# Layer 0's second adaLN round moved from TensorE to two VectorE accumulators

## The chip, the cores and the metric

The kernel runs as one program on one core of one Trainium2 chip. The metric is the device time of one execution in microseconds (us), as the median of several executions. Of the core's engines four matter here: TensorE (PE, matrix products into PSUM), VectorE (DVE, elementwise), ScalarE (ACT, elementwise and exponentials), and the SyncE queue (SP), which issues the loads from HBM. Each engine works through its own instruction list in a fixed order; instructions on different engines wait for each other through semaphores.

## The reference

A decoder trunk of two layers over 256 tokens of width 1024. What matters here, cut from the reference:

```python
for l in range(DEPTH):                                  # 2 layers
    mod = jax.nn.silu(c) @ ada_w[l] + ada_b[l]          # c (1, 1024), ada_w (1024, 6144)
    sh_a, sc_a, g_a, sh_m, sc_m, g_m = jnp.split(mod, 6, axis=-1)
    h = x * (1 + sc_a) + sh_a
    parts = jnp.split(h @ w_in[l], SPLIT_POINTS, axis=-1)
    oa = dilated_attention(aq, ak, av, bias_a)                      # group A
    ob, _ = banded_attention(rope(bq), rope(bk), bv, 127, sinks)    # group B
    oc = nsa_attention(cq, ckc, cvc, ..., gates, cmp_w1, cmp_w2)    # group C
    mixed = jnp.concatenate([oa, ob, oc], axis=-1)
    x = layer_norm(DN_ALPHA * x + (1 + g_a) * (mixed @ w_out[l]), ln_g[l, 0], ln_b[l, 0])
    h = x * (1 + sc_m) + sh_m
    f = jnp.square(relu(h @ mlp_w1[l])) @ mlp_w2[l]
    x = layer_norm(DN_ALPHA * x + (1 + g_m) * f, ln_g[l, 1], ln_b[l, 1])
```

`mod` is a vector times a 1024 x 6144 matrix. The kernel computes it in rounds. The round at issue is layer 0's round 2: `sc_m` and `sh_m`, 2048 columns, needed only when the MLP's input `h` is made after the attention.

## The kernel before, in words

**Stages of layer 0.** The input projection runs from the start to about 69 us. Then comes the attention: group C in eight units (0 to 7: one for each half n of the tokens and each pair of heads), its compressed branch (`c` and `C`, fed by `compress`, whose steps are the letter `s`), group B (`b`, `B`) and group A (`E`, `e`), with the remaining projections between them (`a` is the chunk t11, `A` the chunk t13). Then the output projection (`wo`, L1044), a transition that makes the MLP's input, and the MLP. Every weight that is multiplied in full precision is first split into a high and a low part: ACT writes `whi` (L179), DVE writes `wlo` (L180), into the ten buffers of the pool `spl` (tag `w`, L127).

**A unit of attention.** PE makes scores `s` (L680 or L744), DVE adds the bias and takes the extreme (L634), ACT makes exponentials (L636), DVE and ACT scale `P` (L642, L640), PE transposes it (`tp`, L648), ACT copies it out (`pT`, L650), PE multiplies by the values (`acc`), and ACT and DVE write the result's two parts (`mx`, L666 and L667).

**Loads.** `rawload` (L136) takes one of four 1 MB buffers (`raw`, L126) and issues its load on SP. SP issues in program order, so a load whose buffer is not yet free holds up all loads behind it.

**The adaLN rounds.** `gemv` (L202) is a generator. Each step loads 1 MB of the round's weights and multiplies it in. With `dve` set, DVE does it into accumulators of 128 x 1024: the first row block by a tensor-scalar multiplication (L229), each later one by a multiply-add (L234); at the end PE sums the accumulator's 128 partitions with a matmul by ones (L242). Without `dve`, PE does it: four matmuls for each block of 128 rows, each into 32 columns of the array and 512 wide (`gemv_mm`, L167 and L168). Before, layer 0's round 3 (a gate, four steps, one accumulator, `GV[0] = 'v'`) goes to DVE and round 2 (eight steps, `GV[1] = None`) to PE. Both are queued in `fill` (L921), round 3 first.

**What sets the order.** The string `ORDER[0]` lists the attention's jobs by letter; each dot runs one step of the first generator in `fill` (`filler`, L276), and `filler(100)` (L1038) runs what is left. So in layer 0 dots 1 to 4 are the steps of round 3; dot 5 is its end and step 0 of round 2; further dots are the next steps. A list scheduler then lays each engine's instructions out in one fixed order from this, by priorities and its own cost estimates; what stands in that order is printed below in the section on the change.

Of the kernel before, what the change touches and what calls it, by code (L numbers as in the profile page):

```python
# [10 lines left out]
F32 = mybir.dt.float32  # L11
# [8 lines left out]
S, D, DEPTH, FF, N_IN = 256, 1024, 2, 4096, 2584  # L20
# [7 lines left out]
SPARES = (('w', 'P', 'qk'), ('w', 'qk', 'P', 'mx'))  # L28
EARLY = 3
FO = (1, 3)  # L30
ORDER = ('kv0..21s4.3sa5.s.Acb.6.B7C..Ee', '.ts..q0412...ss3s.kva5cb.67AB.E..Ce')
GV = ('v', None, 'v', 'v', 'v')
START = ('r', '', '', '', '', '', 'bpbco', 'b', '')
GROUPS = ((0, 4, 0), (4, 8, 32))

# [85 lines left out]
def trunk_kernel(ctx: ExitStack, tc: tile.TileContext, a):  # L121
# [5 lines left out]
    spl = pool("spl", 10)  # L127
    att = pool("att")
# [73 lines left out]
    def gemv(l, r, dve=None, early=0):  # L202

        gate = r in GATE
        w = 256 if gate else 512
        nk = 2 if gate else 1
        if dve:
            acc = [att.tile([128, D], F32, name="qk", tag="qk", bufs=3) for _ in range(1 if gate else 2)]
        else:
            gv = ps.tile([128, 512], F32, name="gv", tag="pt")  # L210
        ahead = []
# [226 lines left out]
    def load_ln(l, s):  # L438
        t = big.tile([128, 2, D], F32, name="lnb", bufs=1)
        for i, k in enumerate(("ln_g", "ln_b")):  # L440
            src = a[k]
            nc.sync.dma_start(t[:, i], bass.AP(tensor=src.tensor, offset=src.offset + (2 * l + s) * D,
                                               ap=[[0, 128], [1, D]]))
        return t
# [474 lines left out]
    for l in range(DEPTH):  # L919
        nc.vector.tensor_scalar(nsink[l], pp("sink", 4 * l, 4), -1.0, None, op0=OP.mult)  # L920
    fill += [gemv(0, 3, GV[0]), gemv(0, 2, GV[1])]  # L921

    for l in range(DEPTH):
# [66 lines left out]
        else:  # L990
# [6 lines left out]
            def rows(w, dst, scale, step=1):  # L997

                def run(b):
                    t = u2("kr")[:, :256]  # L1000
                    nc.scalar.activation(t, v_tile(w, b, 256), AF.Copy, scale=scale)
                    tp = ps.tile([128, 4, 128], F32, name="tp", tag="acc")
                    for i in range(2):
                        nc.tensor.transpose(tp[:, i], t[:, i * 128:(i + 1) * 128], ident)
                    return lambda: nc.scalar.activation(dst[:, :, b * 128:(b + 1) * 128][:, :, ::step], tp[:, :2], AF.Copy)
                return run

            end = finish((l, 1), before, SPARES[1], (lambda b: vc_out(b, v_tile(ws, b, NVC)), rows(wk, KK, 1.0),
                                                     rows(wq, qC[:, 0:2], QS, -1)))
            fill.append(gemv(1, 3, GV[2]))  # L1010
            with tc.issue_after(end[1]):
                for n in end[2]:
# [22 lines left out]
        jobs["+"] = lambda: next(btab)  # L1035
        for j in ORDER[l]:
            jobs[j]()
# [39 lines left out]
        def m1_rows(g, b):  # L1077

            if b == 0:
                FT[g] = new_f()  # L1080
            o = v_tile(W1[g], b, 256)
            t = u2("fr")
            nc.scalar.activation(t[:, :256], o, AF.Relu)
            nc.scalar.activation(t[:, 256:], t[:, :256], AF.Square)
            tp = ps.tile([128, 4, 128], F32, name="tp", tag="acc")
            for i in range(2):
                nc.tensor.transpose(tp[:, i], t[:, 256 + i * 128:384 + i * 128], ident)
            ts = slice(b * 128, (b + 1) * 128)

            def parts_out():  # L1090
                nc.scalar.activation(FT[g][:, 0, :, ts], tp[:, :2], AF.Copy)
                nc.vector.tensor_tensor(FT[g][:, 1, :, ts], tp[:, :2], FT[g][:, 0, :, ts].bitcast(F32), op=OP.subtract)
            return parts_out
# [14 lines left out]
        def m2(g, b, hs):  # L1108
            f = FT[g]
            t = slice(b * 128, (b + 1) * 128)  # L1110
            for i, h in ((i, h) for i in range(2) for h in hs):
# [9 lines left out]
        end = transition(lambda b, h: [wo(b, c2, h) for c2 in (2, 3)], accs, ROUND[l, 3], lnb, (l, 2), before, SPARES[0],  # L1121
                         [lambda b, g=g: m1_rows(g, b) for g in range(EARLY)])
        fill.append(gemv(l, 4, GV[3]))
        if l == 0:
            fill += [gemv(1, 1, GV[4]), gemv(1, 2, GV[4])]
        lnb = load_ln(l, 1)
# [90 lines left out]
```

## Time and profile before

| | |
|---|---|
| median of 3 executions | 706.01 us (705.96 to 706.22) |
| the profiled execution: its time | 706.43 us |
| the profiled execution: its span, first to last instruction | 704.7 us |
| mean granted TensorE clock | 0.991 of 2.4 GHz |
| attention of layer 0, up to the first `wo` matmul | about 69 us to 156.1 us |

The profile comes from one execution. It gives for each engine its busy time, the chain of work that ended last (followed back from the last instruction through what released each step), the instructions in order of time, and the clock that TensorE was granted. The modelled end of a matmul overlaps the next one's start, so the distance between two starts is the better price of a matmul.

### The profile page before, as it was taken

What the parts mean: (1) busy time and instruction counts of PE and PEld (TensorE: products, weight loads), DVE (VectorE), ACT (ScalarE), POOL (GpSimd) and SP (SyncE); (2) the same over time, 40 slices, a digit from 0 to 9 for tenths busy, and PEclk for the clock granted to TensorE, in tenths of its full rate; (3) what the DMA queues carried; (4) which work ended last, traced back from release to release, by engine and by line L of the source; (5) the groups of instructions that cost most, each with busy time, mean ns of one, the idle gap of its engine ahead of it and who ended that gap; (6) DMA issues with size and microseconds to landing.
All of it is one profiled execution on the core that took longest, in us unless ns stands there. A gap on an engine that the chain in (4) does not pass through costs nothing.

```text
span 704.7 us, 11146 instructions
## 1 busy us (share of the span) xinstructions
PE 674.1 (96%) x4284; PEld 550.9 (78%) x4284; DVE 492.3 (70%) x947; ACT 402.6 (57%) x781; POOL 39.1 (6%) x39
## 2 busy tenths in 40 slices
PE   5998899999999999999998999999999999999994
PEld 4898658458788888888878977867788888888883
DVE  3455965657799879798977976657779855555556
ACT  2345473785665546656555447598474655656550
POOL 0000000000400000000013020000220000000003
PEclk9999999999999999999999999999999999999998
DMA  9998686568459989798873757710538955555501
GB/s 337 350 353 312 224 319 231 169 236 312 162 183 363 346 309 344 283 344 327 326 262 120 282 226 274 272 39 23 183 117 294 373 214 195 212 183 180 180 0 60
DMA packets 29553, 167.68 MB, mean 238 GB/s; under 512 B 3199, under 2 KB 6683, under 8 KB 11964
## 3 DMA queue, kind: packets, MB, share of 16 engines
q1 hardware_dynamic: 29436, 166.94, 65.0%
q8 instruction: 34, 0.56, 0.3%
q14 instruction: 19, 0.16, 0.1%
q0 software_dynamic: 64, 0.02, 0.0%
HBM read 165.87 MB, written 1.08 MB: 237 GB/s over the span
## 4 chain that ended last, share of the span: by engine, by line
PE 89%; DVE 4%; ACT 3%; issue 1%; POOL 1%; DMA 1%; SPq 0%; POOLq 0%; DVEq 0%
PE mm L368 14%; PE m L1116 8%; PE m L1117 8%; PE m L1118 8%; PE mmv L385 7%; PE mm L369 7%; PE s L680 3%; PE tp L648 3%; PE gv L168 3%; PE mm L355 2%; PE mm L357 2%; PE mm L356 2%; PE wo L1051 2%; PE wo L1053 2%; PE acc L696 2%; PE wo L1052 2%
## 5 line engine op out<-in xcount | busy, mean ns | idle before, releaser
L180 DVE TENSOR_TENSOR wlo<-raw,whi 128x1024 fp32r<-128x1024 f32 (+2 forms) x166 | 196.8, 1203 | 56.5 <-ACT whi L179 54.9
L179 ACT ACTIVATE whi<-raw 128x1024 fp32r<-128x1024 f32 (+2 forms) x175 | 179.2, 1041 | 56.8 <-PE wo L1052 17.2
L368 PE MATMUL mm<-hT,whi 128*128 128x512 f32 x416 | 148.3, 398 | 0.0
L369 PE MATMUL mm<-hT,wlo 128*128 128x256 f32 x416 | 117.0, 281 | 0.9 <-DVE wlo L180 0.9
L1116 PE MATMUL m<-whi,mx 128*128 128x512 f32 x256 | 100.1, 391 | 0.0
L1117 PE MATMUL m<-wlo,mx 128*128 128x512 f32 x256 | 100.0, 391 | 0.0
L1118 PE MATMUL m<-whi,mx 128*128 128x512 f32 x256 | 99.5, 390 | 0.0
L368 PEld LDWEIGHTS mm<-hT,whi 128*128 128x128 f32 x416 | 78.2, 188 | 20.3 <-ACT whi L179 0.8
L369 PEld LDWEIGHTS mm<-hT,wlo 128*128 128x128 f32 x416 | 78.5, 189 | 2.5 <-DVE wlo L180 1.6
L234 DVE SCALAR_TENSOR_TENSOR qk<-raw,se,qk 128x1024 f32<-128x1024 f32 x56 | 71.4, 1286 | 2.5 <-DMA raw<-in_ada_dram 1.9
L371 ACT ACTIVATE P<-mm 128x256 f32<-128x256 f32 x52 | 19.7, 378 | 73.0 <-PE mm L369 73.0
L385 PE MATMUL mmv<-whi,hT 128*128 128x256 f32 (+2 forms) x352 | 55.9, 304 | 4.7 <-ACT hT L466 4.7
L1116 PEld LDWEIGHTS m<-whi,mx 128*128 128x128 f32 x256 | 48.1, 188 | 11.2 <-ACT whi L179 0.8
L1118 PEld LDWEIGHTS m<-whi,mx 128*128 128x128 f32 x256 | 48.1, 188 | 10.1
L1117 PEld LDWEIGHTS m<-wlo,mx 128*128 128x128 f32 x256 | 48.0, 188 | 8.9
L385 PEld LDWEIGHTS mmv<-whi,hT 128*128 128x128 f32 x352 | 48.8, 194 | 6.9 <-ACT hT L466 5.9
L636 ACT ACTIVATE P<-P,sxt 128x128 f32<-128x128 f32 (+1 forms) x96 | 42.6, 446 | 17.2 <-DVE sxt L634 17.0
L355 PE MATMUL mm<-hT,whi 128*128 128x256 f32 x128 | 37.4, 292 | 0.0
L357 PE MATMUL mm<-hT,wlo 128*128 128x256 f32 x128 | 37.0, 289 | 0.0
L356 PE MATMUL mm<-hT,whi 128*128 128x256 f32 x128 | 36.8, 287 | 0.0
L634 DVE CUSTOM_DVE_ANT_0 P<-s,bias 128x128 f32<-128x128 f32 (+1 forms) x80 | 25.7, 351 | 14.4 <-PE s L680 12.0
L1103 DVE TENSOR_TENSOR mx<-P,mx 128x512 fp32r<-128x512 f32 x26 | 17.9, 690 | 25.6 <-ACT mx L1102 25.6
(215 smaller groups left out, 1090.4 us busy)
## 6 DMA issues: line engine op xcount, KB each, us to landing
raw<-in_mlp_w_dram SPq DMA_DIRECT2D x64, 1024.0 KB, 6.5
raw<-in_ada_dram SPq DMA_DIRECT2D x32, 1024.0 KB, 5.9
raw<-in_adag_dram SPq DMA_DIRECT2D x16, 1024.0 KB, 6.7
raw<-in_w_in_dram SPq DMA_DIRECT2D x9, 1024.0 KB, 6.1
raw<-in_cmp_w_dram SPq DMA_DIRECT2D x8, 1024.0 KB, 6.8
raw<-in_w_out_dram SPq DMA_DIRECT2D x8, 1024.0 KB, 6.8
w<-in_w_in_dram SPq DMA_DIRECT2D x8, 396.0 KB, 7.2
w<-in_w_in_dram SPq DMA_DIRECT2D x8, 384.0 KB, 6.1
```

The source lines that it names most:

```text
L179: nc.scalar.activation(hi, t, AF.Copy)
L180: (eng or nc.vector).tensor_tensor(lo, t, hi.bitcast(F32), op=OP.subtract)
L234: nc.vector.scalar_tensor_tensor(ac, src, by, ac, op0=OP.mult, op1=OP.add)
L355: nc.tensor.matmul(o[:, i], hi[:, c], hT[:, 0, kc], start=kc == 0, stop=False, skip_group_check=True)
L356: nc.tensor.matmul(o[:, i], hi[:, c], hT[:, 1, kc], start=False, stop=False, skip_group_check=True)
L357: nc.tensor.matmul(o[:, i], lo[:, c], hT[:, 0, kc], start=False, stop=kc == KC - 1, skip_group_check=True)
L368: nc.tensor.matmul(o, hi[:, c], hT[:, :, kc], start=kc == 0, stop=False, skip_group_check=True)
L369: nc.tensor.matmul(o[:, 0], lo[:, c], hT[:, 0, kc], start=False, stop=kc == KC - 1, skip_group_check=True)
L385: nc.tensor.matmul(o, hT[:, x_, kc, t], ws[kc][w_], start=kc == 0 and x_ + w_ == 0, stop=kc == KC - 1 and w_ == 1)
L1116: nc.tensor.matmul(o, f[:, 0, i, t], hi[:, s], start=first, stop=False)
L1117: nc.tensor.matmul(o, f[:, 0, i, t], lo[:, s], start=False, stop=False)
L1118: nc.tensor.matmul(o, f[:, 1, i, t], hi[:, s], start=False, stop=lastk)
```

## The change

Round 2 of layer 0 goes to DVE as well. Its two accumulators (`av`) are taken from the ten weight buffers of `spl`, since the tag `qk` has three buffers that are in use. The dots of `ORDER[0]` are spread: nine before, fifteen now, one or two after nearly every job, of which thirteen are used up by the two rounds.

```diff
-ORDER = ('kv0..21s4.3sa5.s.Acb.6.B7C..Ee', '.ts..q0412...ss3s.kva5cb.67AB.E..Ce')
-GV = ('v', None, 'v', 'v', 'v')
+ORDER = ('kv0..2.1.s4.3.s.a5..s.A.cb.6.B7.C.Ee', '.ts..q0412...ss3s.kva5cb.67AB.E..Ce')
+GV = ('v', 'v', 'v', 'v', 'v')
...
         if dve:
-            acc = [att.tile([128, D], F32, name="qk", tag="qk", bufs=3) for _ in range(1 if gate else 2)]
+            if (l, r) == (0, 2):
+                acc = [spl.tile([128, D], F32, name="av", tag="w") for _ in range(2)]
+            else:
+                acc = [att.tile([128, D], F32, name="qk", tag="qk", bufs=3) for _ in range(1 if gate else 2)]
```

Line numbers of the changed kernel are three higher from here on (L234 becomes L237). Below, the instruction orders of the two kernels at three places.

First SP's list of loads in the attention, before. `cmp_w` is what `compress` multiplies (two loads for each of its two passes), `adag` the weights of round 3, `ada` those of round 2, `w_in` the chunks t11 and t13.

```order
L138 DMA raw<-in_cmp_w_dram 128x2048 x2
L138 DMA raw<-in_adag_dram 128x2048
L138 DMA raw<-in_cmp_w_dram 128x2048 x2
L138 DMA raw<-in_w_in_dram 128x2048
L138 DMA raw<-in_adag_dram 128x2048
L138 DMA raw<-in_ada_dram 128x2048
L138 DMA raw<-in_w_in_dram 128x2048
L138 DMA raw<-in_ada_dram 128x2048 x2
L250 DMA abg<-in_abg_dram 128x1x256
L138 DMA raw<-in_ada_dram 128x2048
```

The same list of the changed kernel, from the same place.

```order
L138 DMA raw<-in_adag_dram 128x2048 x2
L138 DMA raw<-in_cmp_w_dram 128x2048 x2
L138 DMA raw<-in_ada_dram 128x2048 x2
L138 DMA raw<-in_cmp_w_dram 128x2048 x2
L253 DMA abg<-in_abg_dram 128x1x256
L138 DMA raw<-in_ada_dram 128x2048
L257 DMA gd_1145<-rs 4x256
L138 DMA raw<-in_w_in_dram 128x2048
L259 DMA G<-gd_1145 128x1024
L138 DMA raw<-in_ada_dram 128x2048 x3
L138 DMA raw<-in_w_in_dram 128x2048
L138 DMA raw<-in_ada_dram 128x2048 x2
```

The adaLN loads now stand ahead of the loads of both passes of `compress`, and the chunks t11 and t13 stand behind three and six of round 2's loads instead of none and one.

Then PE around the end of the second pass of `compress` (`cp`, then `hid`), before. `mm<-hT` are the 48 matmuls of t11, `cv` and `sc` the compressed keys and their scores.

```order
L812 MATMUL cp<-raw,F 32x256 x5
L696 MATMUL acc<-pT,vc 64x128 x8
L818 MATMUL hid<-co,cpt 128x32 x2
L680 MATMUL s<-KK,qk 128x512
L648 MATMUL tp<-p_78,P 128x128 x2
L355 MATMUL mm<-hT,whi 128x256
L648 MATMUL tp<-p_78,P 128x128
L356 MATMUL mm<-hT,whi 128x256
L648 MATMUL tp<-p_78,P 128x128
L680 MATMUL s<-KK,qk 128x512
L357 MATMUL mm<-hT,wlo 128x256
```

The same place of the changed kernel.

```order
L699 MATMUL acc<-pT,vc 64x128 x4
L815 MATMUL cp<-raw,F 32x256 x8
L821 MATMUL hid<-co,cpt 128x32 x2
L683 MATMUL s<-KK,qk 128x512 x2
L841 MATMUL cv<-gK,p_81 64x16 x4
L848 MATMUL cv_1351<-p_81,gV 128x64 x2
L708 MATMUL sc<-KCT,qk 128x32 x4
L651 MATMUL tp<-p_78,P 128x128
L358 MATMUL mm<-hT,whi 128x256
L359 MATMUL mm<-hT,whi 128x256
L651 MATMUL tp<-p_78,P 128x128 x5
L360 MATMUL mm<-hT,wlo 128x256
```

The matmuls of t11 stood between `hid` and `cv`; now they stand behind `cv` and `sc`.

Last DVE, from the split of t11 on, before: `cs` and `sx` are the softmax of the compressed branch, `PC` its result.

```order
L849 SCALAR_TENSOR_TENSOR vcr<-cv_1315,co 128x512
L180 TENSOR_TENSOR wlo<-raw,whi 128x1024 x2
L713 TENSOR_TENSOR cs<-sc,co 128x8x15
L714 TENSOR_REDUCE sx<-cs 128x8
L715 TENSOR_TENSOR cs<-cs,sx 128x8x15
L717 TENSOR_TENSOR cs<-cs,co 128x8x15
L718 TENSOR_REDUCE sx<-cs 128x8
L719 TENSOR_SCALAR sx<-sx 128x8
L720 RECIPROCAL sx<-sx 128x8
L252 SCALAR_TENSOR_TENSOR rs<-rs,abg 128x256
L721 TENSOR_TENSOR sx<-sx,gt 128x8
L724 TENSOR_TENSOR PC<-cs,sx 128x8x15
```

The same chain of the changed kernel; `av` are round 2's steps.

```order
L180 TENSOR_TENSOR wlo<-raw,whi 128x1024
L718 TENSOR_TENSOR cs<-cs,sx 128x8x15
L720 TENSOR_TENSOR cs<-cs,co 128x8x15
L237 SCALAR_TENSOR_TENSOR av<-raw,se,av 128x1024 x2
L721 TENSOR_REDUCE sx<-cs 128x8
L722 TENSOR_SCALAR sx<-sx 128x8
L723 RECIPROCAL sx<-sx 128x8
L724 TENSOR_TENSOR sx<-sx,gt 128x8
L237 SCALAR_TENSOR_TENSOR av<-raw,se,av 128x1024 x2
L852 SCALAR_TENSOR_TENSOR vcr<-cv_1351,co 128x512
L727 TENSOR_TENSOR PC<-cs,sx 128x8x15
L237 SCALAR_TENSOR_TENSOR av<-raw,se,av 128x1024 x2
```

Four multiply-adds now stand inside the chain that ends in `PC`, and two right behind it. The whole round, two L232 and fourteen L237 instructions on `av`, stands ahead of the instruction that scales `P` of job `b`.

## Rows read from the trace of the kernel before

**Rows 1.** The page's busy times (engine, us, share, instructions), and its chain by engine.

```profile
PE 674.1 (96%) x4284; PEld 550.9 (78%) x4284; DVE 492.3 (70%) x947; ACT 402.6 (57%) x781; POOL 39.1 (6%) x39
PE 89%; DVE 4%; ACT 3%; issue 1%; POOL 1%; DMA 1%; SPq 0%; POOLq 0%; DVEq 0%
```

**Rows 2.** The chain that ended last, 110 to 157 us: shares by line, then pieces (start, us).

```profile
by line: PE gv L168 24.6%; PE tp L648 13.3%; PE s L744 10.9%; PE s L680 9.1%; PE acc L696 7.3%; PE mm L357 4.7%; PE acc L731 4.6%; PE mm L355 4.5%; PE mm L356 4.3%; PE acc L763 3.7%; PE sc L705 3.7%; DVE P L634 1.8%; PE cv L845 1.6%; PE gv 
...
113.76 0.86 PE gv L168 x8
...
122.74 0.97 PE gv L168 x2
...
124.81 0.99 PE gv L168 x6
...
155.12 0.99 PE gv L168 x6
```

**Rows 3.** Stretches: length, then busy us of PE, PEld, DVE, ACT, POOL; PEclk, DMA share, GB/s.

```profile
92.15:100.84 8.69, 8.69 (x78) 4.83 (x78) 4.25 (x27) 7.21 (x24) 0.00 (x0) 1.00 0.99 371
100.84:125.13 24.29, 24.29 (x194) 19.15 (x197) 15.69 (x50) 12.43 (x35) 0.00 (x0) 1.00 0.67 243
125.13:132.00 6.87, 6.87 (x34) 2.19 (x28) 3.12 (x13) 4.08 (x14) 0.00 (x0) 1.00 0.43 154
132.00:144.00 12.00, 11.93 (x70) 5.67 (x68) 7.55 (x39) 8.47 (x28) 0.00 (x0) 1.00 0.60 187
144.00:156.00 12.00, 11.96 (x87) 5.92 (x84) 6.72 (x28) 10.77 (x31) 0.00 (x0) 1.00 0.47 175
```

**Rows 4.** Lines 229 and 234 on DVE: count, least/median/most ns, first and last start.

```profile
L229 DVE TENSOR_SCALAR qk<-raw,se x8: 742/747/749, 78.0 to 528.8; 128x1024 f32<-128x1024 f32 x8
L234 DVE SCALAR_TENSOR_TENSOR qk<-raw,se,qk x56: 1180/1278/1786, 79.0 to 553.0; 128x1024 f32<-128x1024 f32 x56
```

**Rows 5.** DVE in order of time (start, us, what).

```profile
92.15 0.42 DVE L634 CUSTOM_DVE_ANT_0 P<-s,bias 128x256 f32<-128x256 f32 x1 [0.44 <-PE s L680]
...
95.78 0.61 DVE L642 TENSOR_SCALAR P<-P,sxt 128x256 f32<-128x256 f32 x2
...
100.84 0.23 DVE L820 COPY u<-hid 128x64 f32<-128x64 f32 x1 [0.23 <-PE hid L818]
...
106.51 1.28 DVE L234 SCALAR_TENSOR_TENSOR qk<-raw,se,qk 128x1024 f32<-128x1024 f32 x1
107.70 0.61 DVE L642 TENSOR_SCALAR P<-P,sxt 128x256 f32<-128x256 f32 x2
...
125.13 0.29 DVE L642 TENSOR_SCALAR P<-P,sxt 128x128 f32<-128x128 f32 x1
```

**Rows 6.** SP's issues in order of time (start, us, what).

```profile
80.25 0.33 SPq L138 DMA_DIRECT2D raw<-in_adag_dram  x1
84.39 3.92 SPq L138 DMA_DIRECT2D raw<-in_cmp_w_dram  x2
```

**Rows 7.** Loads by source, 60 to 160 us: count, KB each, median us to landing.

```profile
raw<-in_ada_dram SPq DMA_DIRECT2D x8, 1024.0 KB, 4.8
```

**Rows 8.** The page's group of ACT's splits (count, then busy us, mean ns).

```profile
L179 ACT ACTIVATE whi<-raw 128x1024 fp32r<-128x1024 f32 (+2 forms) x175 | 179.2, 1041 | 56.8 <-PE wo L1052 17.2
```

**Rows 9.** The chain, 60 to 200 us: start, us, what.

```profile
156.11 0.43 PE wo L1051
156.54 0.23 PE wo L1052
...
161.72 0.58 PE tp L261 x4
```

**Rows 10.** PE's first matmul after its wait at 58 us.

```profile
59.65 1.55 PE L331 MATMUL mm<-hT,whi 128*128 128x256 f32 x5 [1.62 <-ACT hT L309]
```

**Rows 11.** Two stretches, columns as in rows 3.

```profile
60.00:64.00 4.00, 3.87 (x20) 3.66 (x19) 2.75 (x4) 1.70 (x3) 0.00 (x0) 0.57 0.49 157
...
76.00:78.00 2.00, 1.05 (x5) 0.47 (x3) 2.00 (x5) 0.09 (x1) 0.00 (x0) 1.00 0.50 94
```

## The prediction

> **What bounds the kernel now.** I read the page's chain first. PE is busy 96% of the span and holds 89% of the chain, DVE 70% and 4% [rows 1], so in general work that leaves PE for DVE should gain. But these are averages, and the round at issue lies in one stage. So I next read the chain of that stage, from 110 to 157 us: the line of round 2's matmuls (L168) holds 24.6% of it [rows 2], that is 0.246 x 47 = 11.6 us. This is the most that can be gained. Then I read the stretches [rows 3]: PE is busy all the time from 92 to 156 us, DVE and ACT are not. DVE has 4.4 us free of 8.7 before 100.84, and 8.6 us of 24.3 up to 125.13. ACT is at 10.77 of 12 us in the last stretch. The reader is to see two things there: in the middle of the attention there is room on DVE, about as much as the change wants; at its end ACT has hardly any.
>
> **What leaves PE.** 32 matmuls (64 records, two for each) go. They stand in the chain in 12 pieces, from 113.76 to 155.12 us, nearly all 0.97 to 0.99 us long [rows 2]. A piece of two records costs 0.97 us and a piece of eight 0.99, so what counts is the number of pieces. The Trainium skill (TensorE: Matmul & The Clock Gate, Part 3 on row and column tiling) says that matmuls in different column strips run at once, so that four cost little more than one. By that, eight steps would cost 7.9 us. The trace agrees for a step that stays together; it has 12 pieces for eight steps because the order cuts steps apart. By the rule alone the sum below would be some 3 us higher; I go by the rows. From 125.13 on, the sum needs 9.4 us of the 11.6: the pieces before it are 0.86 and 0.97, and 0.32 of the third [rows 2].
>
> **What comes to PE.** Four matmuls by ones, 512 wide in four column strips: one piece like those above, 1.0 us.
>
> **What comes to DVE.** Two tensor-scalar multiplications at 0.75 us and fourteen multiply-adds [rows 4]. The next instruction starts 1.19 us after a multiply-add (106.51 to 107.70) [rows 5], so the price is 14 x 1.2 + 2 x 0.75 = 18.3 us. By the order, all of them stand ahead of the instruction that scales P of job b, which ran at 125.13 before [rows 5]. They are spread less than the dots say: the scheduler has them done by there. Two multiply-adds of round 3, which ran behind 100.84 before (one is the row at 106.51 [rows 5]), have moved forward ahead of the second pass of compress, 2.4 us. From 92.15 to 125.13, a stretch of 33.0 us, DVE was busy 4.25 + 15.69 = 19.9 us [rows 3]. It now has 19.9 + 18.3 - 2.4 = 35.8 us to do. So even if it never waited it would come 2.8 us late. DVE takes PE's place as what bounds this stretch, and it works in order: softmax steps wait behind multiply-adds, and PE and ACT wait for the softmax.
>
> **How late DVE is at that instruction.** I laid the loads and the instructions of this stretch out by hand, in the new order, with the durations of the rows.
> Up to the second pass of compress: the second load of the first pass of compress must wait for a buffer that round 3's second step frees, at 84.4 us, which is when SP could issue the next load before as well [rows 6]. At 4.8 us to landing [rows 7] it is there at 89.2. Before, that load had been issued ahead of the adag load at 80.25 [rows 6]. With two more multiply-adds ahead, the first scores of the next unit reach DVE at 93.8, not 92.15 [rows 5]. Two new tensor-scalars stand among them; P is scaled at 97.5, not 95.78 [rows 5]. PE transposes P at 98.6 and has nothing before it, since the loads of the second pass now stand behind those of round 2: SP issues the first at 91.4, behind one of round 2, and it lands at 98.8 (at 371 GB/s [rows 3] a load of 1.05 MB takes 2.8 us, and the queue is full). Then come round 3's sum and the sixteen matmuls of the pass. DVE's copy of its result (L820) is at 105.6, not 100.84 [rows 5]: **+4.8 us**.
> From there: 15.69 us of work [rows 3], less the 2.4 us that moved, plus twelve multiply-adds (14.4 us), is 27.7 us, and I allow 0.7 us for two waits, on ACT's exponential and on the parts of the compressed branch. Before it took 24.3 us. **+4.1 us.** t11's load comes at 107.8, so its matmuls no longer fill PE's wait for the compressed keys; that is within this sum, since DVE is what goes on.
> So the instruction at 125.13 comes at about 134.0: **+8.9 us**.
>
> **The rest of the attention.** Before, it took 31.0 us from 125.13 to the first wo matmul at 156.11 [rows 9], of which 9.4 us go and 1.0 us comes: 22.6 us, if PE went on as before. But the pieces of round 2 stood in gaps in which PE would have waited for ACT. ACT had 4.08 + 8.47 + 10.77 = 23.3 us of work there [rows 3], of which one split of 1.04 us [rows 8] moves behind: 22.3 us. In its fullest stretch before, ACT was 90% busy (10.77 of 12 [rows 3]); at that share it needs 24.8 us, so **+2.2 us** stay. If ACT were fed without a gap it would be 0, and if none of the freed gaps closed, 8.4.
> Some work is done early by then: six wo matmuls at 0.23 us and the four transposes of round 2's result (0.58 us) [rows 9], **-2.0 us**.
>
> **Edits that I cost at nothing.** The two accumulators leave eight weight buffers, four splits in flight; t11 and t13 need two splits each, and their matmuls stand ahead of nearly all of w_out's splits in the order. If that cover failed, one split on ACT and one on DVE would stand in the chain, some 2.2 us (1.04 us on ACT [rows 8] and the like on DVE). The last two dots run nothing. After the transition the orders of PE, DVE and ACT are the same as before; only a few loads swap places in the MLP, where DVE's rounds are covered by PE's matmuls.
>
> **Sum.** +8.9 - 9.4 + 1.0 + 2.2 - 2.0 = +0.7 us. The profiled execution took 706.43 us (span 704.7), 0.4 us above the median of 706.01; so the profile after would read 707.1, and the median 706.7 us. The gain of PE is given back by DVE and ACT.
>
> **Rivals.**
> *DVE keeps up: faster.* Its waits before, 13 us of 33, were waits for PE and ACT; the multiply-adds may fill just these. For it: 35.8 us of work against 33.0 is a shortfall of 2.8 us only, and my layout by hand puts it at 8.9 because every wait of one engine is passed to the next. Against it: the order puts four multiply-adds inside the short chain that ends in PC, and loads of compress behind those of round 2. With half of my delay (+4.5) and half of ACT's (+1.1): 4.5 - 9.4 + 1.0 + 1.1 - 2.0 = -4.8, or 701.2 us; at the ends of both (2.8 and 0) it is -7.6, 698.4 us.
> *The clock falls in PE's new gaps: slower.* Before, a wait of 1.62 us at 58 us [rows 10] was followed by 4 us at a granted clock of 0.57 [rows 11], near the lower level of 1.2 GHz: 4 x 0.43 = 1.7 us of matmul time lost. Another half-empty stretch, 76 to 78 us, kept 1.00 [rows 11], so it need not happen. By my layout PE gets three gaps of 2.3 to 4 us: ahead of the second pass of compress, ahead of cv, and ahead of PC. If it falls in each: 3 x 1.7 = +5.1, or 711.8 us. It decides against the kernel from the first fall on. The Trainium skill (TensorE: Matmul & The Clock Gate, HAM oscillation) says that gaps between matmuls put the array back to half its clock each time; the row at 58 us agrees, the one at 76 us does not.
> *The accumulators hold up splits of w_out.* The 2.2 us above: 708.9 us. It would show as ACT's L179 waiting for the matmuls by ones. I count it with the second.
>
> **Chances and range.** That gain and loss cancel, with 704 to 710 as its own range: 0.42. That DVE keeps up: 0.33. That the clock or the buffers cost more: 0.25. A measurement of this kernel can tell about 0.2%, 1.4 us, from no change. Below 704.6 lies nearly all of the second case and a little of the first, 0.37; within 1.4 us 0.23; above 707.4 a third of the first and nearly all of the third, 0.40. The range of 700.5 to 711.8 leaves out the ends of the second case, and clock losses beyond three falls.
>
> **What would show it.** In the profile after: DVE over 90% busy from about 95 to 134 us; L820's second copy near 105.6 us and the scaling of P of job b near 134, against 100.84 and 125.13; PE with gaps ahead of the second pass of compress and ahead of cv, and the granted clock after them; ACT near 90% in the last 20 us of the attention; the first wo behind the last compressed unit close to 156 us. I am wrong if DVE reaches b's scaling before 130 us (then it is faster), or if PE waits for ACT's pT and P by more than 2 us in the end (then it is slower).

## The result, and the profile after

The changed kernel takes 715.52 us (median of 4 runs, 714.99 to 718.07), the kernel before 706.12 us beside it: a ratio of 1.014, 95% interval 1.0125 to 1.0155. It is 9.4 us slower. 706.7 was forecast, with a range up to 711.8; the time lies outside of it. The profiled execution took 718.07 us (span 716.3), 2.5 us above the median and 11.6 above the profiled one of before.

The page of the changed kernel, its busy times, answers to [rows 1]:

```profile
PE 674.7 (94%) x4228; PEld 556.3 (78%) x4228; DVE 509.0 (71%) x963; ACT 402.1 (56%) x781; POOL 39.5 (6%) x39
```

PE's busy time has hardly changed, though 64 of its records are gone and 8 have come. DVE has 16.7 us more, about the work that was added. Averages hide where the 11.6 us went; the stretch of the attention shows it. First the kernel before, 84 to 156 us, then the changed one, the same stretch and parts of it (columns as in [rows 3]: length, busy us of PE, PEld, DVE, ACT, POOL, then PE's granted clock, DMA share, GB/s):

```profile
84.00:156.00 72.00, 71.84 (x525) 42.41 (x523) 43.06 (x181) 48.69 (x148) 0.00 (x0) 1.00 0.67 242
```

```profile
84.00:156.00 72.00, 61.65 (x372) 41.34 (x371) 50.94 (x151) 34.10 (x104) 0.00 (x0) 0.81 0.73 266
80.00:84.00 4.00, 4.00 (x16) 4.00 (x15) 4.00 (x12) 1.68 (x5) 0.00 (x0) 0.58 1.01 383
95.00:134.00 39.00, 31.59 (x209) 22.15 (x209) 26.96 (x74) 15.27 (x45) 0.00 (x0) 0.78 0.80 290
95.00:112.40 17.40, 14.23 (x97) 7.05 (x97) 8.38 (x32) 7.68 (x26) 0.00 (x0) 0.80 0.79 284
112.40:143.91 31.51, 25.98 (x137) 20.49 (x138) 28.13 (x63) 12.85 (x34) 0.00 (x0) 0.70 0.79 287
100.00:104.00 4.00, 3.15 (x24) 2.51 (x24) 3.91 (x11) 2.90 (x10) 0.00 (x0) 0.64 0.98 330
104.00:108.00 4.00, 4.00 (x22) 1.23 (x20) 0.49 (x2) 0.96 (x3) 0.00 (x0) 0.51 0.11 34
116.00:124.00 8.00, 6.45 (x35) 6.30 (x36) 6.11 (x20) 4.02 (x9) 0.00 (x0) 0.50 0.61 236
136.00:144.00 8.00, 8.00 (x24) 4.99 (x23) 7.90 (x14) 3.74 (x14) 0.00 (x0) 0.50 0.73 271
156.00:176.00 20.00, 19.84 (x160) 14.38 (x157) 11.80 (x55) 17.95 (x49) 0.00 (x0) 1.00 0.08 21
```

Before, PE is busy 71.84 of 72 us at a granted clock of 1.00. After, it stands idle for 10.35 us, and the mean granted clock of the stretch is 0.81, with 61.65 us busy. An estimate from these two numbers: 0.19 x 61.65 = 11.7 us of matmul time lost to the lower level of 1.2 GHz, which is what the stretches at 0.50 and 0.51 are. Together 22.0 us of PE are missing. Less the 11.6 us of round 2 that PE no longer has to do, and plus 1.0 for the matmuls by ones, that is 11.4 us, against 11.6 measured in the profiled runs. The balance closes to within some 2 us: it leaves out a fall of the clock at 80 to 84 us (0.58, an estimated 0.42 x 4.0 = 1.7 us), where the profile of before has 1.00. The gain was there, and about twice as much was lost on PE. A balance tells where PE's time went, not why.

DVE, which I had made the bound of this part, is busy 26.96 of 39 us between 95 and 134, 69%. The mean hides two halves: up to the second copy of compress, at 112.40, it is busy 8.38 of 17.40 us, and from there to the scaling of P of job b, at 143.91, 28.13 of 31.51, 89%. Its landmarks, as in [rows 5] (start, us, what; in brackets its wait and what ended it):

```profile
96.04 0.42 DVE L637 CUSTOM_DVE_ANT_0 P<-s,bias 128x256 f32<-128x256 f32 x1 [0.83 <-PE s L683]
...
112.40 0.23 DVE L823 COPY u<-hid 128x64 f32<-128x64 f32 x1 [6.18 <-PE hid L821]
...
114.15 2.47 DVE L237 SCALAR_TENSOR_TENSOR av<-raw,se,av 128x1024 f32<-128x1024 f32 x2
...
117.23 0.22 DVE L831 SCALAR_TENSOR_TENSOR gK<-uw,u 128x64 f32<-128x64 f32 x1
...
143.91 0.48 DVE L645 TENSOR_SCALAR P<-P,sxt 128x128 f32<-128x128 f32 x2
```

The first scores of the next unit come at 96.04 (92.15 before), the second copy of compress at 112.40 (100.84 before), the scaling of P of job b at 143.91 (125.13 before). At the second of these DVE had waited 6.18 us for PE, not PE for DVE. SP's issues (answers to [rows 6]) and PE's waits behind them:

```profile
88.93 2.68 SPq L138 DMA_DIRECT2D raw<-in_ada_dram  x2
92.88 0.81 SPq L138 DMA_DIRECT2D raw<-in_cmp_w_dram  x2
...
106.84 0.43 SPq L138 DMA_DIRECT2D raw<-in_w_in_dram  x1
...
109.50 7.48 SPq L138 DMA_DIRECT2D raw<-in_ada_dram  x3
123.67 0.33 SPq L138 DMA_DIRECT2D raw<-in_w_in_dram  x1
```

```profile
98.61 0.67 PE L683 MATMUL s<-KK,qk 64*128 64x256 f32 x2 [0.96 <-DVE sxt L637]
100.31 1.48 PE L651 MATMUL tp<-p,P 128*128 128x128 f32 x8 [1.04 <-DVE P L645]
102.33 1.98 PE L699 MATMUL acc<-pT,vc 128*64 128x128 f32 x16 [0.53 <-ACT pT L653]
...
117.55 0.62 PE L841 MATMUL cv<-gK,p 128*64 128x16 f32 x8 [3.75 <-issue]
...
123.19 0.41 PE L360 MATMUL mm<-hT,wlo 128*128 128x256 f32 x1
...
126.13 0.28 PE L360 MATMUL mm<-hT,wlo 128*128 128x256 f32 x1
...
135.28 2.07 PE L683 MATMUL s<-KK,qk 64*128 64x512 f32 x2 [1.47 <-DVE sxt L637]
```

SP issued the second pair of compress's weights from 84.39 before [rows 6]; now it does so from 92.88, behind two loads of round 3 and two of round 2. t13's load, at 123.67, stands behind three more of round 2. On PE there are waits of 0.96, 1.04 and 0.53 us ahead of the second pass, then 3.75 ahead of cv and 1.47 behind PC. At each group the clock falls: a matmul of 256 columns takes 0.41 us at 123.19 and 0.28 at 126.13.

None of these waits ends at a load; where the profile names what ended one, it is DVE or ACT. The second pair's first load landed 7.0 us after its issue, at 99.9, and the pass begins at 105.08; t11's landed 4.8 us after 106.84, at 111.6, and its first matmul runs at 120.79. So, as I read it, the late loads act through the fixed order: the matmuls that multiply them stand further back, and the softmax waits that they used to fill are left open. For the longest wait, 3.75 us ahead of cv, the profile names no other engine (`issue`); but cv needs `gK`, which DVE writes at 117.23 behind two of round 2's multiply-adds (114.15), and cv starts at 117.55.

### The profile page after: what moved, and what is told of

The parts are those of the page before. It is cut to its first block, busy times and chain, and to the rows that moved or that the text cites. A ratio compares the mean times of both kernels' runs of the same rounds, so it can differ in the third digit from the quotient of the medians.

```text
span 716.3 us, 11053 instructions
## 1 busy us (share of the span) xinstructions
PE 674.7 (94%) x4228; PEld 556.3 (78%) x4228; DVE 509.0 (71%) x963; ACT 402.1 (56%) x781; POOL 39.5 (6%) x39
## 4 chain that ended last, share of the span: by engine, by line
PE 87%; DVE 6%; ACT 3%; issue 2%; DMA 1%; POOL 1%; SPq 0%; POOLq 0%; DVEq 0%; ACTq 0%
PE mm L371 14%; PE m L1119 8%; PE m L1120 8%; PE m L1121 8%; PE mmv L388 7%; PE mm L372 7%; PE s L683 3%; PE tp L651 3%; PE mm L358 2%; PE mm L360 2%; PE mm L359 2%; PE wo L1054 2%; PE wo L1056 2%; PE wo L1055 2%; PE acc L699 2%; PE mm L334 2%
## 5 line engine op out<-in xcount | busy, mean ns | idle before, releaser
L372 PE MATMUL mm<-hT,wlo 128*128 128x256 f32 x416 | 117.0, 281 | 0.9 <-DVE wlo L180 0.9
L237 DVE SCALAR_TENSOR_TENSOR qk<-raw,se,qk 128x1024 f32<-128x1024 f32 x56 | 71.2, 1282 | 0.3
L358 PE MATMUL mm<-hT,whi 128*128 128x256 f32 x128 | 39.3, 307 | 0.0
L360 PE MATMUL mm<-hT,wlo 128*128 128x256 f32 x128 | 38.8, 303 | 0.0
L359 PE MATMUL mm<-hT,whi 128*128 128x256 f32 x128 | 38.4, 300 | 0.0
L1106 DVE TENSOR_TENSOR mx<-P,mx 128x512 fp32r<-128x512 f32 x26 | 17.9, 689 | 25.6 <-ACT mx L1105 25.6
L423 POOL TENSOR_TENSOR ve<-ve,co 128x1 f32<-128x1 f32 x8 | 4.4, 553 | 570.0 <-DVE ve L422 356.2
```

The source lines that it names most:

```text
L237: nc.vector.scalar_tensor_tensor(ac, src, by, ac, op0=OP.mult, op1=OP.add)
L358: nc.tensor.matmul(o[:, i], hi[:, c], hT[:, 0, kc], start=kc == 0, stop=False, skip_group_check=True)
L359: nc.tensor.matmul(o[:, i], hi[:, c], hT[:, 1, kc], start=False, stop=False, skip_group_check=True)
L360: nc.tensor.matmul(o[:, i], lo[:, c], hT[:, 0, kc], start=False, stop=kc == KC - 1, skip_group_check=True)
L372: nc.tensor.matmul(o[:, 0], lo[:, c], hT[:, 0, kc], start=False, stop=kc == KC - 1, skip_group_check=True)
```

## The experiments

Four theories were to be told apart. **DVE**: the added multiply-adds make all that stands behind them in DVE's queue late. **Loads**: the new row of dots puts loads of rounds 3 and 2 ahead of weights that PE waits for (compress, t11, t13), whatever engine works on the round. **Clock**: PE's new gaps let its clock fall, and that is most of the loss. **Amount**: only the sum of PE's work counts. Each kernel below was timed beside the kernel before on the same chip; that had medians of 706.1 to 706.2 us throughout.

**The two halves of the change, each alone.** The change does two things: the round goes to DVE, and the row of dots is another. First the new round with the old dots.

```diff
-ORDER = ('kv0..2.1.s4.3.s.a5..s.A.cb.6.B7.C.Ee', ...
+ORDER = ('kv0..21s4.3sa5.s.Acb.6.B7C..Ee', ...
```

> The changed round on DVE, with the old row of dots (two dots fewer, steps later and closer together). If the early steps of round 2 in front of the second compress pass are what makes everything late, L823's second copy comes back to some 105 us and the time to 706 to 711 us. If it is the amount of work on DVE or the number of loads whatever their place, 714 to 718 us.

Measured: 703.20 us, ratio 0.9959 (0.9938 to 0.9981), below both of the ranges that I had set. It is faster than both kernels: the round on DVE, which I had priced at a wash, gains 2.9 us. Its stretch of the attention, and the end of it:

```profile
84.00:156.00 72.00, 68.04 (x508) 46.66 (x507) 59.67 (x200) 50.20 (x154) 0.00 (x0) 0.95 0.71 258
140.00:156.00 16.00, 13.15 (x85) 8.98 (x82) 14.22 (x39) 10.33 (x31) 0.00 (x0) 0.79 0.66 226
```

SP's issues of t11 and t13 before; then in this run the second pair of compress, t11 and t13; then the two landmarks on DVE:

```profile
89.96 0.33 SPq L138 DMA_DIRECT2D raw<-in_w_in_dram  x1
...
99.25 0.33 SPq L138 DMA_DIRECT2D raw<-in_w_in_dram  x1
```

```profile
85.23 3.91 SPq L138 DMA_DIRECT2D raw<-in_cmp_w_dram  x2
90.80 0.33 SPq L138 DMA_DIRECT2D raw<-in_w_in_dram  x1
...
100.08 0.33 SPq L138 DMA_DIRECT2D raw<-in_w_in_dram  x1
```

```profile
101.68 0.23 DVE L823 COPY u<-hid 128x64 f32<-128x64 f32 x1 [0.23 <-PE hid L821]
...
126.81 0.28 DVE L645 TENSOR_SCALAR P<-P,sxt 128x128 f32<-128x128 f32 x1
```

The second pair of compress is issued from 85.23, t11 at 90.80, t13 at 100.08, each 0.8 us later than before (84.39, 89.96 and 99.25). The copy is 0.8 us later than before and job b's scaling 1.7, with the first multiply-adds of round 2 ahead of it. Some idle time and a low clock are left behind 140 us.

Then the other half, the old round on TensorE with the new dots.

```diff
-ORDER = ('kv0..21s4.3sa5.s.Acb.6.B7C..Ee', ...
+ORDER = ('kv0..2.1.s4.3.s.a5..s.A.cb.6.B7.C.Ee', ...
```

(here against the kernel before)

> The kernel before with nothing changed but the row of dots: round 2 stays on TensorE. Theory load order (the new dots put round 3's and round 2's loads ahead of compress's, and PE stands empty behind them, whatever engine does round 2): 711 to 719 us, that is 5 to 13 us slower than before, with gaps on PE ahead of the compress passes. Theory that only both halves of the change together hurt (DVE late and loads early): 704 to 708 us.

Measured: 713.92 us, ratio 1.0109 (1.0087 to 1.0132): 7.8 us slower, without one new instruction on DVE. The stretch, and the landmarks on DVE:

```profile
84.00:156.00 72.00, 66.52 (x474) 42.09 (x473) 39.51 (x158) 40.45 (x119) 0.00 (x0) 0.93 0.77 287
```

```profile
111.21 0.23 DVE L820 COPY u<-hid 128x64 f32<-128x64 f32 x1 [5.98 <-PE hid L818]
...
140.03 0.48 DVE L642 TENSOR_SCALAR P<-P,sxt 128x128 f32<-128x128 f32 x2
```

The copy comes at 111.21 and job b's scaling at 140.03, 10.4 and 14.9 us later than before, nearly as late as in the changed kernel. So lateness of this kind is there without DVE's work, and so are PE's three waits ahead of the second pass (0.96, 1.13 and 0.53 us in this trace). How much can't be read here, since the new dots also moved PE's pieces of round 2: of their 64 records 16 start ahead of the copy and 48 ahead of the scaling, none and about a dozen before, an estimated 3 and 5 us of PE's own work. The four corners: 706.1 (old round, old dots), 703.2 (new round), 713.9 (new dots), 715.5 (both). With the old dots the round gains 2.9; with the new ones it gains nothing (1.6 us slower, and the runs of the old round lie between 712.31 and 715.92). The dots cost 7.8 or 12.3.

**Loads without the work, and work without the loads.** What is it in the new dots? First the multiply-adds of round 2 cut to 8 columns, with all loads in place.

```diff
-  nc.vector.scalar_tensor_tensor(ac, src, by, ac, op0=OP.mult, op1=OP.add)
+  w8 = 8 if (l, r) == (0, 2) else D
+  nc.vector.scalar_tensor_tensor(ac[:, :w8], src[:, :w8], by, ac[:, :w8], op0=OP.mult, op1=OP.add)
```

> The changed kernel, but the 14 multiply-adds of round 2 run over 8 columns of 1024 (the rest of round 2's sum is left out), so that DVE has some 15 us less to do while every load, wait, buffer and the place of each step stay. Theory DVE (its 18 us of new work make everything behind it late; the falls of the clock are a consequence of the gaps that this leaves on PE): the loss goes and the freed 9.4 us of PE show, 701 to 705 us, b's P scaled before 130 us. Theory loads (round 2's loads now stand ahead of those of compress, t11 and t13, and PE's gaps come from there): 712 to 716 us, the gaps ahead of the second compress pass and ahead of cv remain, with the low clock after them. A mixed cause gives 706 to 711.

Measured: 711.39 us (708.60 to 712.30), ratio 1.0067 (1.0047 to 1.0088). The stretch, PE's wait ahead of cv, and the two landmarks on DVE:

```profile
84.00:156.00 72.00, 65.24 (x432) 44.85 (x430) 42.36 (x180) 43.48 (x129) 0.00 (x0) 0.83 0.73 271
```

```profile
112.25 0.62 PE L842 MATMUL cv<-gK,p 128*64 128x16 f32 x8 [1.63 <-issue]
```

```profile
109.22 0.23 DVE L824 COPY u<-hid 128x64 f32<-128x64 f32 x1 [4.18 <-PE hid L822]
...
126.03 0.47 DVE L646 TENSOR_SCALAR P<-P,sxt 128x128 f32<-128x128 f32 x2
```

DVE has 42.36 us of work, less than before, and PE is still idle for 6.8 us at a mean clock of 0.83. The numbers lie at the edge of the mixed case: freeing DVE gives back 4.1 us of the 12.3 that the dots cost. The copy is 8.4 us later than before, without DVE's work. The wait ahead of cv is 1.63 us, not 3.75, so the multiply-adds made some of it. Job b's scaling comes at 126.03, 0.9 us later than before and 17.9 earlier than in the changed kernel: "before 130 us", the sign that theory DVE had set, came true, and the kernel is 5.3 us slower than before all the same. So DVE's work does make that instruction late, but the time does not follow from it.

Next the contrary: DVE's 16 instructions stay, on a resident tile, and the eight loads are left out.

```diff
-  t = ahead[st] if st < len(ahead) else load(st)
+  t = x.rearrange("p b d -> p (b d)") if (l, r) == (0, 2) else ahead[st] if st < len(ahead) else load(st)
```

> The changed kernel, but round 2's steps multiply a resident tile in place of their weights, so that its eight loads are left out (and with them round 2's true sum) while DVE's 16 instructions stay. Theory DVE: 712 to 717 us, as the changed kernel. Theory loads: 700 to 706 us, PE's gaps ahead of the second compress pass and cv gone and the clock at 1.00 there.

Measured: 703.27 us (701.24 to 711.28, ten runs that scatter widely), ratio 0.9978 (0.9943 to 1.0013).

```profile
84.00:156.00 72.00, 67.75 (x503) 47.64 (x501) 61.62 (x203) 49.62 (x149) 0.00 (x0) 0.98 0.48 171
```

DVE is at 61.62 us, fuller than in the changed kernel, and yet the loss is gone: 12.2 us less than the changed kernel. Theory DVE by itself falls; without the eight loads where the new dots put them there is no loss. The run also takes their 8.4 MB off the queues, lets DVE work ahead and has its order planned anew; the next runs keep every load.

**Which dots.** Only the early ones (..2.1.s, loads of round 3 ahead of the first pair of compress) or only the late ones (from unit 4 on), each with the round on DVE (the first of the two lines with a plus, and the second):

```diff
-ORDER = ('kv0..2.1.s4.3.s.a5..s.A.cb.6.B7.C.Ee', ...
+ORDER = ('kv0..2.1.s4.3sa5.s.Acb.6.B7C..Ee', ...
+ORDER = ('kv0..21s4.3.s.a5..s.A.cb.6.B7.C.Ee', ...
```

> The round on DVE, the two early dots of the changed kernel (in ..2.1.s), and the old dots behind them. If the early dots are what costs: 711 to 717 us. If it is the dots around the second pass of compress: 701 to 706.

> The round on DVE, with the old dots ahead of unit 4 and the new ones behind it: against the changed kernel the two early dots (in ..2.1.s) are gone, so the loads of the first compress pass stand ahead of round 3's last two again, while those still stand ahead of the second pass. If the two early dots are what costs: 700 to 705 us. If one load ahead of the second pass of compress costs as much: 710 to 716. In between if each costs its part.

Measured: early dots alone 705.49 us, ratio 0.9977 (0.9955 to 0.9998); late dots alone 712.53 us, ratio 1.0085 (1.0070 to 1.0100). Their stretches, early first:

```profile
84.00:156.00 72.00, 66.26 (x471) 45.44 (x469) 57.40 (x195) 46.71 (x144) 0.00 (x0) 0.95 0.70 259
```

```profile
84.00:156.00 72.00, 63.06 (x427) 45.07 (x427) 55.28 (x174) 41.16 (x124) 0.00 (x0) 0.86 0.73 272
```

Both times lie in the range that blames the dots around the second pass, not those ahead of the first. The early dots cost 2.3 us over the run with the old ones, the late dots 9.3; the sum is 11.6, and both together cost 12.3. That the second pass of compress comes later is paid for cheaply: with the early dots alone its copy on DVE runs at 108.55, 7.7 us later than before. What tells the two runs apart I can't read from SP's issues alone. t11's, the early dots first:

```profile
94.49 0.33 SPq L138 DMA_DIRECT2D raw<-in_w_in_dram  x1
```

```profile
96.96 0.33 SPq L138 DMA_DIRECT2D raw<-in_w_in_dram  x1
```

t13 follows at 107.69 and at 110.88. The late dots have them 2.5 and 3.2 us later, and the run is 7.0 us slower; in its trace PE waits 3.1 us for t11's split on ACT and 3.0 us for a softmax on DVE.

Of these the ones behind the second pass alone:

```diff
-ORDER = ('kv0..2.1.s4.3.s.a5..s.A.cb.6.B7.C.Ee', ...
+ORDER = ('kv0..21s4.3s.a5..s.A.cb.6.B7.C.Ee', ...
```

> The round on DVE, the old dots up to the second pass of compress, and the new ones only behind it, so that no load of compress stands behind one of the two rounds that did not before, while round 2's steps are spread wider than with the old dots. By the theory of load order it has the gain of the moved round without the loss: 700 to 703 us, at or below the run with the old dots (703.2). By the theory that spreading round 2 among the softmax steps is itself what makes DVE late: 705 to 712.

Measured: 707.99 us, ratio 1.0001 (0.9969 to 1.0033), in ten runs from 700.74 to 710.06: three at 700.74 to 701.44, seven at 707.41 to 710.06. The median lies in the range of the theory of spreading, the three short runs in that of theory loads, so the run decides for neither. By its median it is 4.8 us slower than the old dots, and the late dots ahead of the second pass cost 4.5 more. In the profile SP issues t13 behind three loads of round 2, where the old dots had one; but the profiled run took 701.44 us, so t13's late load by itself is not the loss. The longer outcome has no profile, and its cause stays open. The issue and the stretch of the profiled run:

```profile
106.86 0.33 SPq L138 DMA_DIRECT2D raw<-in_w_in_dram  x1
```

```profile
84.00:156.00 72.00, 66.85 (x499) 46.78 (x498) 61.28 (x200) 49.70 (x152) 0.00 (x0) 0.95 0.74 273
```

Then all of round 2 behind t13, and crowded into the last units:

```diff
+ORDER = ('kv0..21s4.3sa5.sA..c.b.6.B7.C.Ee', ...
```

> The round on DVE, with all of round 2's loads behind those of t11 and t13 and its steps crowded into the last units (sA..c.b.6.B7.C). Theory load order: 699 to 703 us, with PE free of gaps up to 125 us. Theory that DVE's work in the last units makes softmax late whatever the loads: 704 to 710, with the loss of time behind 125 us.

Measured: 703.56 us, ratio 0.9969 (0.9957 to 0.9981), between the two ranges. DVE has as much to do here as anywhere (60.46 us), in a shorter time, and there is no loss against the old dots; nor a gain. Both theories show in the trace: PE has no long gap up to 122 us, and then it waits 3.45 us for DVE's `PC`, with two of round 2's multiply-adds in the chain that makes it.

```profile
84.00:156.00 72.00, 65.17 (x496) 45.47 (x494) 60.46 (x200) 50.15 (x152) 0.00 (x0) 0.95 0.73 270
```

```profile
127.58 0.48 PE L729 MATMUL tp<-p,PC 128*128 128x128 f32 x1 [3.45 <-DVE PC L727]
```

**The clock.** The changed kernel, with the old round's 32 matmuls issued as well, into a tile that nobody reads:

```diff
+  if (l, r) == (0, 2):
+      gx = ps.tile([128, 512], F32, name="gx", tag="pt") if k == 0 else gx
+      for j in range(4):
+          gemv_mm(gx, t, kc, j, (k * 4 + j) * w, w, True, True)
```

> The changed kernel, with the 32 small matmuls of the old round issued as well, step by step, into a PSUM tile that nobody reads. PE gets up to 11.6 us of work more, DVE nothing. Theory clock (most of the 9.4 us lost is matmul time at the low clock, and it falls because PE stands empty): the pieces fill some gaps, the granted clock between 100 and 148 us is higher than in the changed kernel, and the time is 708 to 714 us in spite of the work. Theory that the gaps alone count (what PE does in a gap costs nothing and gives nothing): 715 to 717. Theory that PE still bounds the stage: 718 to 725.

Measured: 715.90 us, ratio 1.0138 (1.0115 to 1.0160), the same as the changed kernel.

```profile
84.00:156.00 72.00, 64.64 (x456) 39.75 (x459) 54.35 (x158) 37.25 (x111) 0.00 (x0) 0.93 0.77 286
```

PE carries 11.6 us of work more by the price of [rows 2] and the time is unchanged. The mean clock of the stretch rises from 0.81 to 0.93, so by the same estimate 4.5 us are lost to it, not 11.7, and the idle time falls from 10.35 to 7.4: 10.2 us back. The clock rose as theory clock had it, but the time is the one that the theory of the gaps alone had forecast (715 to 717), not 708 to 714. Either the fed array gives back just what the feeding costs, or the time hangs on the waits, whatever PE does in them; a balance of PE's time can't tell these apart. What the time would be with the gaps and without the falls can't be had from this run, since it changes both.

Repeated runs of one program speak on the same point. With the dots behind the second pass, the three shortest of the ten runs (700.74 to 701.44 us) had a mean granted clock of 0.987 to 0.991, the other seven (707.41 to 710.06) 0.976 to 0.981. With the early dots, three runs at 0.993 took 701.81 to 702.35 us, and those at 0.982 and 0.983 took 708.32 and 706.43. The instructions and their order are the same in all of them. This is a correlation: a later load could both lengthen a run and make a gap in which the clock falls.

**Versions that beat both.** In the run with the old dots, PE was idle for 2.85 us behind 140 and its clock fell. Two edits aimed at that. One dot more, behind the job of t13, so that the round is folded and its two accumulators come free earlier:

```diff
-ORDER = ('kv0..21s4.3sa5.s.Acb.6.B7C..Ee', ...
+ORDER = ('kv0..21s4.3sa5.s.A.cb.6.B7.C.Ee', ...
```

> The round on DVE with the old dots and one more, behind the job of t13 (s.A.cb in place of s.Acb): no weight that PE waits for stands behind a load of round 2 that did not before, and round 2's sum is folded earlier, so that w_out's splits get the two accumulators' buffers sooner. Theory load order: no loss, and some of PE's idle time at the attention's end goes: 700 to 703 us. Theory that any wider spread costs (DVE): 704 to 710.

Measured: 702.27 us (700.78 to 702.31 in five runs), ratio 0.9934 (0.9918 to 0.9950). It is the lowest median of all, but its interval overlaps that of the old dots (0.9938 to 0.9981). Behind 140 us PE is idle for 2.44 us instead of 2.85, and its clock does not fall:

```profile
84.00:156.00 72.00, 67.56 (x512) 45.61 (x512) 59.46 (x199) 51.20 (x153) 0.00 (x0) 1.00 0.71 259
140.00:156.00 16.00, 13.56 (x99) 8.47 (x98) 15.02 (x45) 13.49 (x37) 0.00 (x0) 1.00 0.67 243
```

And the round divided, the old dots:

```diff
...
+  if half and kc == 4:
+      gv = ps.tile([128, 512], F32, name="gv", tag="pt")
+      for j in range(4):
+          nc.tensor.matmul(gv[32 * j:32 * j + 32, :w], ones, acc[j * w // D][:, j * w % D:j * w % D + w],
+                           start=True, stop=False, ...)
-  if dve:
+  if dve and not (half and kc >= 4):
...
```

> The old dots, and round 2 divided: its first four steps on DVE, folded into the round's PSUM tile by the matmuls with ones, its last four on TensorE as before. Theory clock: the pieces in the last units keep PE fed where the run with all of round 2 on DVE showed the low clock (144 to 152 us), so its runs scatter less and lie at a granted clock of 0.99 or more: 700 to 703 us. Theory that only PE's amount of work counts: half of the gain of the whole round, 704 to 705 us.

Measured: 703.13 us (703.02 to 703.16), ratio 0.9954 (0.9942 to 0.9967), between the two ranges and so no decision between them. PE is full to the end and five runs agree within 0.14 us, where those with the old dots and the whole round on DVE lie between 700.1 and 706.4:

```profile
84.00:156.00 72.00, 70.67 (x542) 45.47 (x542) 51.70 (x197) 51.92 (x154) 0.00 (x0) 1.00 0.70 256
140.00:156.00 16.00, 15.78 (x107) 7.95 (x106) 7.05 (x27) 11.23 (x28) 0.00 (x0) 1.00 0.59 208
```

Both at once:

> Both edits that gained by themselves: round 2 divided between DVE (first four steps) and TensorE (last four), and the one dot more behind the job of t13. If the two gains come from different idle time of PE and add up (3.1 and 0.9 us): about 702 us, with as little scatter as the divided round had. If the extra dot only frees the accumulators of a round that is wholly on DVE, it brings nothing here: 703.

Measured: 705.76 us, ratio 0.9988 (0.9979 to 0.9997). The gains don't add, they cancel, and neither reading forecast that.

```profile
84.00:156.00 72.00, 70.58 (x527) 45.68 (x526) 50.05 (x190) 49.09 (x150) 0.00 (x0) 0.98 0.67 242
```

PE has as much busy time in the stretch as in the divided round by itself (70.58 against 70.67). The clock, 0.98 against 1.00, accounts for an estimated 1.4 of the 3.0 us between the two profiled runs (706.05 and 703.02). Why the rest is lost was not settled. The eleven runs lie between 703.34 and 706.38 us, so an array that is hardly idle does not by itself make the runs agree.

## Why the prediction was wrong

**The step that failed** is "How late DVE is at that instruction", and with it that the time would follow from that instruction. +8.9 us was forecast for the scaling of P of job b, and it came 18.8 us late. Its two terms fared differently. Up to the copy of compress, +4.8 was forecast and +11.6 measured, and here the mechanism was wrong: DVE is busy 8.38 of 17.40 us and waits for PE. From the copy on, +4.1 was forecast and +7.2 measured (31.5 us instead of 24.3), and here "DVE takes PE's place as what bounds this stretch" nearly held: DVE is busy 28.13 us, 27.7 forecast, but waits 3.4 where 0.7 was allowed. That the time hangs on it is what the run with the small multiply-adds refutes: the scaling is on time there (126.03), and the kernel still 5.3 us slower than before.

**What stands in its place.** The loads came nearly as I laid them out: the second pair of compress was issued at 92.88 (91.4 forecast) and its first load landed at 99.9 (98.8). From that landing to the copy I allowed 6.8 us, and it took 12.5, in softmax waits of PE and at half clock; a part of the copy's lateness, an estimated 1.7 us, is the clock's fall at 80 to 84 us, which came before all this. I did not count what the new order does to PE: 10.35 us of idle time, since nothing else stands in its waits, and an estimated 11.7 us at the lower clock. My sum held no term for the clock. I wrote that t11's late load "is within this sum, since DVE is what goes on"; at cv DVE was indeed what PE waited for, but PE's idle time and the clock behind it were not in the sum.

**The second rival** (the clock falls in PE's new gaps) had the right sign and nearly the right places: ahead of the second pass, ahead of cv, and behind PC where I had it ahead of PC. It was priced at three falls of 1.7 us, 5.1 in all, from the one fall at [rows 10, 11]. Measured are some 11.7 us in the profiled run: the gaps come one behind the other, and from 116 to 124 and from 136 to 144 the clock stays at the lower level for 8 us and more, not 4. The Trainium skill (TensorE: Matmul & The Clock Gate, HAM oscillation) says that an array left waiting for DMA between groups of matmuls runs them at half clock each time. The trace has the half clock from 104, 116 and 136 us (0.51, 0.50, 0.50), but the waits ahead of it ended at DVE and ACT, not at a load.

**What was right.** The gain on PE: the balance above closes with the 11.6 us of [rows 2] less 1.0, and with dots that hold no such weight up it shows as 2.7 to 4.0 us net (three runs with the whole round on DVE). The end of the attention: ACT is at 17.95 of 20 us from 156 to 176, the 90% that were forecast, and PE at 19.84 of 20, so ACT is not what made it late. From job b's scaling to the last wo matmul it took 50.5 us (143.91 to 194.44) instead of 56.9 (125.13 to 182.04): -6.4 us against -8.2 forecast. The first rival, that DVE keeps up and the kernel gains, is what happens once the loads stand where they did. The third (the accumulators hold up w_out's splits) did not show in the changed kernel as ACT waiting; that one earlier dot gains 0.9 us over the old dots would fit it, but that is not clear of the scatter. Neither of the two signs of being wrong that I had named came: DVE was not at b's scaling before 130 us, and from 156 to 176 us PE is idle for 0.16 us. Both looked at DVE and at the end of the attention, and the loss lies on PE in its middle.

**What stays open.** How the 12.3 us that the dots cost divide between idle time and clock, as causes: the two come together in every run. How they divide among the steps: freeing DVE gives back 4.1 us and leaving out the loads all of them, while the late dots ahead of the second pass cost about 4.5 us and those behind it 4.8, in seven runs of ten. And by which way: each of these edits also moves other instructions, since the order is planned anew, so that a late load and the order that was planned around it were never changed one without the other.

## What to carry to other kernels

When a change moves a step in a hand-written order, first list the loads that the step issues and the loads that they now stand ahead of, and only then count its arithmetic; two kernels, one with the old code in the new places and one with the new code in the old places, tell the halves apart. A wait of PE may cost the matmuls behind it half their clock as well, as it did here; it need not (with one dot more, 4.4 us of idle time in the stretch and a clock of 1.00). And of two changes made as one, the half that gains can be hidden by the half that loses: here 2.9 us by 12.3.

## What the runs showed of the hardware

Behind waits of 0.96, 1.04 and 0.53 us, from 98 to 102 us, the granted clock fell to 0.64 and then 0.51, though none was as long as the 1.62 us of [rows 10]; I had looked for single long gaps. The clock also differs from run to run of one program, by 0.976 to 0.991 as a mean over 700 us, and 9.3 us of time go with it; with the divided round (PE busy 70.67 of 72 us) five runs agreed within 0.14 us, but with 70.58 us (the divided round and one dot more) eleven runs were 3.0 us apart, so a full array is not the whole reason.
